# Sums of quarters of h from kept norm products, four more seven-product blocks, and one modulation vector computed a section earlier, in a two-layer hybrid decoder trunk

## The chip, the cores and the metric

The kernel runs on one core of one Trainium2 chip. A core has a matrix engine (TensorE, "PE" in the profile), a vector engine (VectorE, "DVE"), ScalarE ("ACT"), GpSimd ("POOL") and a sync engine ("SP") that here only issues DMAs. Each engine works through its own instructions in program order, and semaphores hold it where it needs another engine's result. The metric is the device time of one execution in microseconds (us).

## What is computed

Two decoder layers of 1024 features over 512 tokens, in float32, and a last norm. Each layer is a feed-forward half step, a mixer and another feed-forward half step; every one of the six has a norm with a shift and a scale that come from the conditioning vector `c`:

```python
mod = (cond @ ada_w[i] + ada_b[i]).reshape(bn, N_SUBLAYERS, 3, D_MODEL)
h = modulate(rms_norm(x, ffn_norm[i, 0]), mod[:, 0, 0], mod[:, 0, 1])   # h*(1+scale)+shift
x = x + 0.5 * mod[:, 0, 2][:, None, :] * swiglu(h, w_gate, w_up, w_down)
# swiglu: (silu(h @ w_gate) * (h @ w_up)) @ w_down, 1024 -> 2816 -> 1024
```

The mixer of layer 0 is a convolution module, that of layer 1 pooling and block attention. The change touches the four feed-forwards. They are called l0s0, l0s2, l1s0 and l1s2 here, after layer and place in the layer. There are 18 modulation vectors of 1024, each a product of `cond` with 4 MB of `ada_w`.

## The kernel before

**Products.** TensorE takes operands of a shorter float (`fp32r`). A float32 product is made from three: each operand is split into an upper part (`whi`, `hh`, `th`) and a rest (`wlo`, `hl`, `tl`), and `mac` (lines 302 to 304) multiplies upper by upper, upper by rest, rest by upper. Weights come by DMA into `raw`; ScalarE casts the upper part (line 284, `whi`) and VectorE subtracts (line 286, `wlo`). In the convolution module some items carry the flag `by_dma`: there ScalarE writes the upper part of `-w` into `wlo` (line 289), and GpSimd issues a DMA that adds `w` to it (line 290), so that VectorE has nothing to do. An *item* is 128 output features over all 512 tokens: for gate and up 8 x 3 = 24 matmuls of 512 columns.

**Sections and blocks.** The 22 blocks of 128 hidden features are done in sections of 8, 6 and 8: gate and up products of a section, then its share of the down product, which is added to `x` (line 1010). A gate block and its up block are two items. Some of them, the last ones of their section, are done together as a *pair* instead: h is cut in quarters (features by tokens), and seven products of quarter size take the place of eight (`pair_run`, `seventh`, line 791), 7 x 12 = 84 matmuls of 256 columns. The numbers of pairs in the three sections are (0, 2, 8) in l0s0, (2, 6, 8) in l0s2, (2, 4, 8) in l1s0 and (2, 6, 8) in l1s2. A pair needs sums of its weights' quarters (`sums13`, `sum2`, `sum4`, their splits; the first pair's are made ahead, in `lead_in`), a few steps on its results, and four sums of quarters of h, which `forms` makes once for each feed-forward, for `kk` = 0 to 3: two additions `hh + hl` of 512 columns into `s13` (line 730) give h back, four steps of 256 columns make the sums (lines 734 to 737), and ScalarE and VectorE split them (lines 741 and 742).

**Modulation vectors.** One vector takes four loads of 1 MB, on VectorE one TENSOR_SCALAR (line 485) and seven SCALAR_TENSOR_TENSOR (line 487) of 128x1024 into `adaacc`, a fold (two transposes and two reductions, lines 500 and 501), one small matmul and `put_mod`. These steps are a list `bg`; `slack` and `beside` put them between items, by estimated costs: each item adds a credit (`free` less the cost of what else stands beside it), and a step is placed when the credit covers it. What is left at the end is done there. `steps` builds the list of a feed-forward.

**Boundaries.** Between two steps, `boundary` takes the last two down items of the old step, the norm and the first items of the new one (the next three or four, whose operands are split early), by halves of 256 tokens. VectorE adds each finished output into `x` (line 1010) and its square into `acc` (line 543); when all eight are in, TensorE sums `acc` over the partitions (`stats`, line 553), and after VectorE and GpSimd have made the scale from that, TensorE spreads it (line 564). `apply` then makes, for each of eight row blocks, `t = x * modA * scale` (line 575, in three turning buffers), `hh` from `t + modB` (ScalarE, line 578) and `hl` (VectorE, line 580). The boundary behind l0s2 has number 3.

Of the kernel before, what the change touches and what calls it, by code (L numbers as in the profile page):

```python
# [68 lines left out]
class Trunk:  # L69
    def __init__(self, ctx, tc, a, out):  # L70
        self.ctx, self.tc, self.nc, self.a, self.out = ctx, tc, tc.nc, a, out
        self.plan = []
        self.later, self.held = [], []
        self.pend = None
        self.ending = False
        self.phase = None
        self.free_banks = list(range(8))
        self.bank_no = {}
# [263 lines left out]
    def setup(self):  # L342
# [224 lines left out]
    def apply(self, i, k, sl, rb):  # L567

        nc = self.nc
        n = sl.stop - sl.start  # L570
        if n == S:
            t = self.fp.tile([P, n], F32, name=f"t{n}", tag="qhi", bufs=3)
        else:
            t = self.np_.tile([P, n], F32, name=f"t{n}", tag="t", bufs=3)
        nc.vector.scalar_tensor_tensor(t, self.x[k][:, sl], self.modA[:, i, k:k + 1],  # L575
                                       rb, op0=ALU.mult, op1=ALU.mult)
        b = self.modB[:, i, k:k + 1]
        nc.scalar.activation(self.hh[k][:, sl], t, AF.Identity, bias=b, scale=1.0)  # L578
# [9 lines left out]
    def boundary(self, tail, i, head, switch=True):  # L588
# [74 lines left out]
    def ffn_items(self, l, s):  # L663
# [8 lines left out]
        for n, nf in enumerate(SECTIONS):  # L672
            gu = []
            for fp in range(nf // 2):
# [7 lines left out]
                def up_post(slot):  # L682
                    def go(ps, sl):
# [8 lines left out]
                c0 = (f0 + 2 * fp) * P  # L692
                apart = (l, s, n, fp) == (0, 0, 0, 1)
                sl_ = (2 * fp, 2 * fp + 1)
                g = self.pair(wg[:, :, c0:c0 + 256], ND, [gate_post(q) for q in sl_], rhs=self.h_rhs,
                              apart=apart)
                u = self.pair(wu[:, :, c0:c0 + 256], ND, [up_post(q) for q in sl_], rhs=self.h_rhs,
                              apart=apart)
                gu += [g[0], u[0], g[1], u[1]]
# [24 lines left out]
    def forms(self, kk):  # L724

        nc = self.nc
        h = self.fp.tile([P, 2, S], F32, name="s13", tag="s13", bufs=1)
        for e in range(2):
            k = kk + 4 * e
            nc.vector.tensor_tensor(h[:, e, :], self.hh[k].bitcast(F32), self.hl[k].bitcast(F32), op=ALU.add)  # L730
        b11, b12 = h[:, 0, 0:256], h[:, 0, 256:512]
        b21, b22 = h[:, 1, 0:256], h[:, 1, 256:512]
        t = [self.fp.tile([P, S], F32, name="yy", tag="yy", bufs=2).rearrange("p (a b) -> p a b", a=2) for _ in range(2)]
        nc.vector.tensor_tensor(t[0][:, 0, :], b12, b11, op=ALU.subtract)
        nc.vector.tensor_tensor(t[0][:, 1, :], b22, t[0][:, 0, :], op=ALU.subtract)
        nc.vector.tensor_tensor(t[1][:, 0, :], b12, b22, op=ALU.subtract)
        nc.vector.tensor_tensor(t[1][:, 1, :], b21, t[0][:, 1, :], op=ALU.subtract)
        for e in range(2):
# [229 lines left out]

    def swiglu_pairs(self, secs, pairs, bg, skip, fn=None, due=0):


        self.form, self.credit, self.room = {}, 0.0, len(bg)
        end = len(bg) - due
        forms = [(lambda kk=kk: self.call(lambda: self.forms(kk)), 4.6) for kk in range(4)]
        lead = [list(zip(self.lead_in(ps[0]), (2.5, 1.4, 1.9, 1.2))) if ps else [] for ps in pairs]
        for n, ((gu, down), ps) in enumerate(zip(secs, pairs)):
# [3 lines left out]
            if n == 0 and ps:  # L980
                todo = forms + [(None, 0)] * (len(gu) - 8) + todo
            rest = self.beside(gu, todo, bg, 3.7, len(ps) > 0) if gu else rest
# [18 lines left out]
        self.plan.append(("sync",))  # L1001
        while bg:
            self.call(*bg.pop(0)[:2])
            self.call(self.flush)
# [542 lines left out]
    def build(self):  # L1547
# [97 lines left out]

        bg = steps(1, (0, 1), (0, 0), (0, 2))
        self.swiglu_pairs(g0, self.pair_items(0, 2, (2, 6, 8)), bg, 3)
        self.boundary(g0[-1][1][6:], 3, f[1, 0][0][0][:4], False)
        bg = steps(1, (1, 1), (1, 0), (1, 2), (2, 1))
        self.swiglu_pairs(f[1, 0], self.pair_items(1, 0, (2, 4, 8)), bg, 3, AF.Exp)  # L1650

# [130 lines left out]
```

## Time and profile before

| | us |
|---|---|
| median of 3 runs | 1843.25 |
| lowest and highest | 1841.98, 1844.58 |
| the profiled execution, its own time | 1845.38 |
| its span in the profile | 1843.6 |
| TensorE busy | 1794.6 (97%) |
| VectorE busy | 1411.1 (77%) |
| ScalarE busy | 816.1 (44%) |
| GpSimd busy | 144.5 (8%) |

The profiled execution's own time is its span and 1.8 us around it. All stretches, waits and durations below are read in that one execution. A busy share is an average over the whole program; for each stage the waits and the timeline of that stage say more.

### The profile page before, as it was taken

The page shows a single profiled execution, that of the slowest core. Times are in us where ns is not written, and L with a number is a line of the kernel's source. Part 1 is how long each engine was busy: PE and PEld are TensorE (multiplying, and loading weights), DVE is VectorE, ACT ScalarE, POOL GpSimd, SP SyncE. Part 2 cuts the span into 40 slices and gives each one's busy share as a digit, 9 for nine tenths or more (in the row PEclk, how much of TensorE's full clock was granted, in tenths as well). Part 3 has the DMA queues.
Part 4 walks back from the last instruction along what each step waited for, and adds up shares of the span by engine and source line. Part 5 has one row for each costly group of instructions (what it writes and reads, how often), then busy time and mean ns, then how long its engine had stood idle before and what let it go on. Part 6 is the DMA issues. An engine that isn't in the chain of part 4 may idle for free.

```text
span 1843.6 us, 26711 instructions
## 1 busy us (share of the span) xinstructions
PE 1794.6 (97%) x10730; PEld 1563.4 (85%) x10730; DVE 1411.1 (77%) x2084; ACT 816.1 (44%) x1404; POOL 144.5 (8%) x123
## 2 busy tenths in 40 slices
PE   5999999999999999999999999999999999999998
PEld 3787889988778888989888889998866788898997
DVE  6689879775797869799677787886898586485874
ACT  4322325447754433436344234453545444253543
POOL 2100000005760000000000000000002000000000
PEclk7999999999999999999999999999999999999999
DMA  9585564447752346353423664543462132424321
GB/s 253 164 295 205 172 187 122 138 115 164 166 177 88 115 162 196 123 148 105 160 71 113 218 210 136 145 133 97 134 205 71 54 92 69 114 81 126 92 92 46
DMA packets 275940, 255.93 MB, mean 139 GB/s; under 512 B 5628, under 2 KB 254312, under 8 KB 275816
## 3 DMA queue, kind: packets, MB, share of 16 engines
q1 hardware_dynamic: 273380, 245.78, 43.5%
q0 software_dynamic: 2304, 8.39, 2.5%
q8 instruction: 84, 1.38, 0.3%
q14 instruction: 40, 0.33, 0.1%
q10 hardware_dynamic: 132, 0.05, 0.0%
HBM read 243.72 MB, written 2.10 MB: 133 GB/s over the span
## 4 chain that ended last, share of the span: by engine, by line
PE 81%; DVE 10%; ACT 3%; issue 2%; POOL 2%; DMA 1%; SPq 0%; ACTq 0%; POOLq 0%; DVEq 0%
PE bank L791 30%; PE bank L302 16%; PE bank L304 16%; PE bank L303 16%; DVE hl L580 1%; DVE wlo L286 1%; DVE adaacc L487 1%; DMA raw<-in_ada_w_dram 1%; ACT whi L284 1%; DVE t L575 1%; POOL y L1124 1%; DVE pm L1362 1%; DVE x L1010 1%; DVE p L1359 0%; DVE acc L1524 0%
## 5 line engine op out<-in xcount | busy, mean ns | idle before, releaser
L302 PE MATMUL bank<-th,whi 128*128 128x512 f32 (+1 forms) x896 | 336.6, 376 | 0.7 <-ACT th L1404 0.7
L304 PE MATMUL bank<-th,wlo 128*128 128x512 f32 (+1 forms) x896 | 333.9, 373 | 2.7 <-POOL wlo L286 2.7
L303 PE MATMUL bank<-tl,whi 128*128 128x512 f32 (+1 forms) x896 | 333.4, 372 | 1.1 <-DVE tl L687 0.9
L302 PE MATMUL bank<-hh,whi 128*128 128x512 f32 (+1 forms) x864 | 322.1, 373 | 5.5 <-ACT hh L578 3.2
L303 PE MATMUL bank<-hl,whi 128*128 128x512 f32 (+1 forms) x864 | 316.6, 366 | 8.1 <-DVE hl L580 8.1
L304 PE MATMUL bank<-hh,wlo 128*128 128x512 f32 (+1 forms) x864 | 315.8, 366 | 3.2 <-DVE wlo L286 2.6
L284 ACT CAST whi<-raw 128x1024 fp32r<-128x1024 f32 (+1 forms) x205 | 204.4, 1012 | 135.8 <-PE bank L303 83.3
L286 DVE TENSOR_TENSOR wlo<-raw,whi 128x1024 fp32r<-128x1024 f32 (+1 forms) x179 | 209.4, 1187 | 19.1 <-ACT whi L284 18.4
L304 PEld LDWEIGHTS bank<-th,wlo 128*128 128x128 f32 x896 | 169.4, 189 | 36.1 <-POOL wlo L286 4.3
L303 PEld LDWEIGHTS bank<-tl,whi 128*128 128x128 f32 x896 | 169.6, 189 | 32.3 <-DVE tl L687 1.3
L302 PEld LDWEIGHTS bank<-th,whi 128*128 128x128 f32 x896 | 169.6, 189 | 32.0 <-ACT th L1404 0.9
L303 PEld LDWEIGHTS bank<-hl,whi 128*128 128x128 f32 x864 | 163.4, 189 | 37.9 <-DVE hl L580 9.6
L302 PEld LDWEIGHTS bank<-hh,whi 128*128 128x128 f32 x864 | 163.6, 189 | 36.9 <-ACT hh L578 3.3
L304 PEld LDWEIGHTS bank<-hh,wlo 128*128 128x128 f32 x864 | 163.7, 189 | 33.2 <-DVE wlo L286 3.7
L1010 DVE SCALAR_TENSOR_TENSOR x<-bank,modG,x 128x512 f32<-128x512 f32 (+1 forms) x124 | 85.7, 698 | 133.2 <-PE bank L304 132.3
L791 PE MATMUL bank<-f,qhi 128*128 128x256 f32 x896 | 165.3, 282 | 0.0
L791 PE MATMUL bank<-f,whi 128*128 128x256 f32 x896 | 163.0, 280 | 0.2
L748 ACT CAST qhi<-raw 128x512 fp32r<-128x512 f32 x168 | 100.7, 621 | 111.9 <-issue 77.1
L487 DVE SCALAR_TENSOR_TENSOR adaacc<-raw,cond,adaacc 128x1024 f32<-128x1024 f32 x112 | 143.7, 1283 | 2.7
L791 PEld LDWEIGHTS bank<-f,whi 128*128 128x128 f32 x896 | 137.6, 188 | 1.9 <-ACT yy L851 0.9
L791 PEld LDWEIGHTS bank<-f,qhi 128*128 128x128 f32 x896 | 138.7, 190 | 0.0
L791 PE MATMUL bank<-f,qlo 128*128 128x256 f32 x448 | 126.5, 282 | 0.2 <-DVE qlo L751 0.2
(247 smaller groups left out, 3334.8 us busy)
## 6 DMA issues: line engine op xcount, KB each, us to landing
raw<-in_ada_w_dram SPq DMA_DIRECT2D x64, 1024.0 KB, 5.0
raw<-in_ffn_w_down_dram SPq DMA_DIRECT2D x32, 1024.0 KB, 5.5
raw<-in_ffn_w_gate_dram SPq DMA_DIRECT2D x58, 512.0 KB, 4.1
raw<-in_ffn_w_up_dram SPq DMA_DIRECT2D x58, 512.0 KB, 5.3
raw<-in_ffn_w_gate_dram SPq DMA_DIRECT2D x15, 1024.0 KB, 5.4
raw<-in_ffn_w_up_dram SPq DMA_DIRECT2D x15, 1024.0 KB, 5.4
raw<-in_ffn_w_down_dram SPq DMA_DIRECT2D x16, 768.0 KB, 4.4
raw<-in_conv_w_in_dram SPq DMA_DIRECT2D x20, 512.0 KB, 5.9
```

The lines of the kernel that those rows point to most:

```text
L284: self.nc.scalar.copy(hi[:, 0:n, :], w)
L286: low = lambda eng=eng, lo=lo, hi=hi, w=w, n=n: eng.tensor_tensor(lo[:, 0:n, :], w, hi[:, 0:n, :].bitcast(F32), op=ALU.subtract)
L302: nc.tensor.matmul(ps, lhsT=it.hi[k], rhs=xh[:, sl], start=start, stop=False)
L303: nc.tensor.matmul(ps, lhsT=it.hi[k], rhs=xl[:, sl], start=False, stop=False)
L304: nc.tensor.matmul(ps, lhsT=it.lo[k], rhs=xh[:, sl], start=False, stop=stop)
L487: nc.vector.scalar_tensor_tensor(acc, r.tile[:, j, :], self.cond[:, k:k + 1], acc, op0=ALU.mult, op1=ALU.add)
L575: nc.vector.scalar_tensor_tensor(t, self.x[k][:, sl], self.modA[:, i, k:k + 1], rb, op0=ALU.mult, op1=ALU.mult)
L580: self.pend = lambda: nc.vector.scalar_tensor_tensor(self.hl[k][:, sl], t, b, self.hh[k][:, sl].bitcast(F32), op0=ALU.add, op1=ALU.subtract)
L748: self.nc.scalar.copy(hi, src)
L791: mm = lambda w, x, start=False: nc.tensor.matmul(ps, lhsT=w, rhs=x, start=start, stop=False, skip_group_check=True)
L1010: nc.vector.scalar_tensor_tensor(self.x[d][:, sl], ps[:, sl], self.modG[:, i, d:d + 1], self.x[d][:, sl], op0=ALU.mult, op1=ALU.add)
L1124: nc.gpsimd.tensor_tensor(y, y, m, op=ALU.add)
```

## The change

1. **Sums from kept products.** In the boundaries to l0s2, l1s0 and l1s2 (`i` = 2, 3, 5) `apply` leaves its eight `t` in buffers that are otherwise the places of the form tiles (`KEPT`). `forms` uses them: h is `t + modB`, so the additions of `hh` and `hl` go, and three of the four sums become SCALAR_TENSOR_TENSOR with `modB`, or with the difference of two of its columns (`modD`, made once). l0s0 stays as it is.
2. **Four more pairs.** l1s0 has (2, 6, 8) and l1s2 has (4, 6, 8).
3. **The order in l1s2's section 0.** With four pairs only 8 items are left there, 3 of which the boundary takes. `joint` puts the forms and the lead-in steps, nine in all, beside the five others.
4. **`by_dma` in l1s2.** The four items of the second weight pair of that section get their lower parts from ScalarE and an adding DMA, as in the convolution module.
5. **One vector in another part.** The scale of layer 1's mixer (vector 1, 1 of layer 1) leaves l1s0's list and joins l0s2's, at its end. What of it is not placed by the end of l0s2 is carried over (`over`).
6. The estimated cost of a form is 3.5 in place of 4.6 where the forms come from kept products.

```diff
+        elif self.keep:
+            if sl.start == 0:
+                self.tt[k] = self.fp.tile([P, S], F32, name=f"t{k}", tag=SPARE[KEPT[k]], bufs=1)
+            t = self.tt[k][:, sl]
...
+        self.call(lambda: (setattr(self, "keep", i in (2, 3, 5)), setattr(self, "fi", i)))
...
+                by_dma = (l, s, n, fp) == (1, 2, 0, 1)
...
+                for it in g + u:
+                    it.by_dma = by_dma
...
+        if self.keep:
+
+            if kk == 0:
+                nc.vector.tensor_tensor(self.modD, self.modB[:, self.fi, 0:4], self.modB[:, self.fi, 4:8],
+                                        op=ALU.subtract)
+            (b11, b12), (b21, b22) = ([self.tt[kk + 4 * e][:, h] for h in HALVES] for e in range(2))
+            b2, bd = self.modB[:, self.fi, kk + 4:kk + 5], self.modD[:, kk:kk + 1]
+            nc.vector.tensor_tensor(t[0][:, 0, :], b12, b11, op=ALU.subtract)
+            for out, x, b, y in ((t[0][:, 1, :], b22, b2, t[0][:, 0, :]), (t[1][:, 0, :], b12, bd, b22),
+                                 (t[1][:, 1, :], b21, b2, t[0][:, 1, :])):
+                nc.vector.scalar_tensor_tensor(out, x, b, y, op0=ALU.add, op1=ALU.subtract)
...
+    def joint(self, forms, lead, n):
+
+        over = len(forms) + len(lead) - n
+        if over <= 0:
+            return forms + lead
+        forms = [forms[:2]] + [[f] for f in forms[2:]]
+        steps = [[f] for f in lead]
+        for e in range(over - 1):
+            steps[e].insert(0, forms.pop(e - over + 1)[0])
...
-                todo = forms + [(None, 0)] * (len(gu) - 8) + todo
+                todo = self.joint(forms + [(None, 0)] * (len(gu) - 8), todo, len(gu))
...
-        while bg:
+        while bg and not over:
...
-        bg = steps(1, (0, 1), (0, 0), (0, 2))
-        self.swiglu_pairs(g0, self.pair_items(0, 2, (2, 6, 8)), bg, 3)
+        bg = steps(1, (0, 1), (0, 0), (0, 2), (1, 1))
+        self.swiglu_pairs(g0, self.pair_items(0, 2, (2, 6, 8)), bg, 3, over=True)
         self.boundary(g0[-1][1][6:], 3, f[1, 0][0][0][:4], False)
-        bg = steps(1, (1, 1), (1, 0), (1, 2), (2, 1))
-        self.swiglu_pairs(f[1, 0], self.pair_items(1, 0, (2, 4, 8)), bg, 3, AF.Exp)
+        bg += steps(1, (1, 0), (1, 2), (2, 1))
+        self.swiglu_pairs(f[1, 0], self.pair_items(1, 0, (2, 6, 8)), bg, 3, AF.Exp)
...
-        self.swiglu_pairs(f[1, 2], self.pair_items(1, 2, (2, 6, 8)), [], 3)
+        self.swiglu_pairs(f[1, 2], self.pair_items(1, 2, (4, 6, 8)), [], 3)
```

The first place where instructions move is the end of l0s2, on VectorE, ahead of boundary 3. `x0_93` to `x7_100` are the eight row blocks of the output, `adaacc` and `yy` belong to the vectors in the list, `acc` to the norm. Before, behind the first output:

```order
L1010 SCALAR_TENSOR_TENSOR x1_94<-bank6_8327,modG_157,x1_94 128x512
L487 SCALAR_TENSOR_TENSOR adaacc_7141<-raw_8127,cond_151,adaacc_7141 128x1024 x2
L543 TENSOR_TENSOR acc_158<-acc_158,sq_8358 128x512
L286 TENSOR_TENSOR wlo_8366<-raw_8246,whi_8365 128x1024
L286 TENSOR_TENSOR wlo_8370<-raw_8246,whi_8369 128x1024
L1010 SCALAR_TENSOR_TENSOR x2_95<-bank7_8373,modG_157,x2_95 128x512
L500 STREAM_TRANSPOSE yy_8404<-adaacc_7141 128x512
L501 TENSOR_REDUCE adar_8403<-yy_8404 128x16
L500 STREAM_TRANSPOSE yy_8407<-adaacc_7141 128x512
L501 TENSOR_REDUCE adar_8403<-yy_8407 128x16
L543 TENSOR_TENSOR acc_158<-acc_158,sq_8399 128x512
L286 TENSOR_TENSOR wlo_8412<-raw_8248,whi_8411 128x1024
```

and from the fifth to the seventh output, whose first half is the last row:

```order
L1010 SCALAR_TENSOR_TENSOR x4_97<-bank1_8448,modG_157,x4_97 128x512
L543 TENSOR_TENSOR acc_158<-acc_158,sq_8474 128x512
L286 TENSOR_TENSOR wlo_8480<-raw_8291,whi_8479 128x1024
L1010 SCALAR_TENSOR_TENSOR x5_98<-bank5_8483,modG_157,x5_98 128x512
L543 TENSOR_TENSOR acc_158<-acc_158,sq_8509 128x512
L524 TENSOR_TENSOR modG_157<-bank3_8511,adabT_150 32x8 x4
L528 TENSOR_SCALAR modG_157<-modG_157 128x8
L286 TENSOR_TENSOR wlo_8520<-raw_8362,whi_8519 128x1024
L1010 SCALAR_TENSOR_TENSOR x6_99<-bank0_8523,modG_157,x6_99 128x256
```

After, behind the first output:

```order
L1048 SCALAR_TENSOR_TENSOR x1_94<-bank6_8313,modG_157,x1_94 128x512
L503 STREAM_TRANSPOSE yy_8347<-adaacc_6273 128x512
L504 TENSOR_REDUCE adar_8346<-yy_8347 128x16
L503 STREAM_TRANSPOSE yy_8350<-adaacc_6273 128x512
L504 TENSOR_REDUCE adar_8346<-yy_8350 128x16
L546 TENSOR_TENSOR acc_159<-acc_159,sq_8344 128x512
L288 TENSOR_TENSOR wlo_8355<-raw_8113,whi_8354 128x1024
L288 TENSOR_TENSOR wlo_8359<-raw_8113,whi_8358 128x1024
L1048 SCALAR_TENSOR_TENSOR x2_95<-bank7_8362,modG_157,x2_95 128x512
L488 TENSOR_SCALAR adaacc_8392<-raw_8232,cond_151 128x1024
L490 SCALAR_TENSOR_TENSOR adaacc_8392<-raw_8232,cond_151,adaacc_8392 128x1024
L490 SCALAR_TENSOR_TENSOR adaacc_8392<-raw_8234,cond_151,adaacc_8392 128x1024 x2
```

and from the fifth to the seventh:

```order
L490 SCALAR_TENSOR_TENSOR adaacc_8392<-raw_8390,cond_151,adaacc_8392 128x1024 x2
L490 SCALAR_TENSOR_TENSOR adaacc_8392<-raw_8395,cond_151,adaacc_8392 128x1024 x2
L546 TENSOR_TENSOR acc_159<-acc_159,sq_8472 128x512
L288 TENSOR_TENSOR wlo_8486<-raw_8399,whi_8485 128x1024
L1048 SCALAR_TENSOR_TENSOR x5_98<-bank3_8489,modG_157,x5_98 128x512
L503 STREAM_TRANSPOSE yy_8518<-adaacc_8392 128x512
L504 TENSOR_REDUCE adar_8517<-yy_8518 128x16
L503 STREAM_TRANSPOSE yy_8521<-adaacc_8392 128x512
L504 TENSOR_REDUCE adar_8517<-yy_8521 128x16
L546 TENSOR_TENSOR acc_159<-acc_159,sq_8515 128x512
L288 TENSOR_TENSOR wlo_8526<-raw_8474,whi_8525 128x1024
L1048 SCALAR_TENSOR_TENSOR x6_99<-bank0_8529,modG_157,x6_99 128x256
```

So two 128x1024 steps and one fold of before (the fold of the third vector) have become eight such steps (the whole fourth vector) and two folds, in the same stretch of TensorE's work, ahead of the norm's sums. Between the two pieces, behind `x3_96`, stand the steps of `modG`, which before stood behind `x5_98`.

The second place is ScalarE in l1s2's section 0, where the last half outputs of the boundary's items (`sg`, `th0_117`) meet the weights of the items behind it. Before:

```order
L578 ACTIVATE hh6_107<-t256_13934,modB_156 128x256
L578 ACTIVATE hh7_108<-t256_13953,modB_156 128x256
L284 CAST whi_13985<-raw_13293 128x1024
L679 ACTIVATE sg_13900<-bank2_13791 128x256
L686 CAST th0_117<-m_14007 128x256
L284 CAST whi_14011<-raw_13350 128x1024
L284 CAST whi_14015<-raw_13604 128x1024
L679 ACTIVATE sg_13912<-bank4_13813 128x256
L284 CAST whi_14023<-raw_13350 128x1024
L686 CAST th1_118<-m_14052 128x512
```

After:

```order
L286 CAST whi_14065<-raw_13378 128x1024
L687 ACTIVATE sg_13984<-bank2_13879 128x256
L694 CAST th0_117<-m_14088 128x256
L286 CAST whi_14092<-raw_13435 128x1024
L291 ACTIVATE wlo_14093<-raw_13435 128x1024
L286 CAST whi_14097<-raw_13690 128x1024
L291 ACTIVATE wlo_14098<-raw_13690 128x1024
L687 ACTIVATE sg_13996<-bank4_13901 128x256
L286 CAST whi_14106<-raw_13435 128x1024
L291 ACTIVATE wlo_14107<-raw_13435 128x1024
L694 CAST th1_118<-m_14136 128x512
```

Three `wlo` steps have come in between, each with a DMA that GpSimd issues behind it; the four subtractions of line 286 are gone from VectorE. Over the whole program TensorE has 192 matmuls of 512 columns fewer and 336 of 256 columns more.

## Rows read from the trace of the kernel before

**Rows 1.** The page: the span, the busy time of each engine (share of the span, instructions), and the chain of work that ended last, by engine.

```profile
span 1843.6 us, 26711 instructions
...
PE 1794.6 (97%) x10730; PEld 1563.4 (85%) x10730; DVE 1411.1 (77%) x2084; ACT 816.1 (44%) x1404; POOL 144.5 (8%) x123
...
PE 81%; DVE 10%; ACT 3%; issue 2%; POOL 2%; DMA 1%; SPq 0%; ACTq 0%; POOLq 0%; DVEq 0%
```

**Rows 2.** The waits of TensorE over the whole span, three groups of the list: the line that waited, what it waited for, us in total, how often, the longest.

```profile
PE bank L303 <- DVE hl L580: 8.1, 6, 1.6
...
PE bank L304 <- POOL wlo L286: 2.7, 1, 2.7
...
PE bank L304 <- DMA wlo<-raw: 0.7, 1, 0.7
```

**Rows 3.** TensorE's timeline in an ordinary item of 24 matmuls of 512 columns: its first matmul and the first one of the next item (start us, duration us, line, operation, output and inputs, shape).

```profile
601.88 0.39 PE L302 MATMUL bank<-hh,whi 128*128 128x512 f32 x1
...
607.48 0.39 PE L302 MATMUL bank<-hh,whi 128*128 128x512 f32 x1
```

**Rows 4.** The chain of work in order of time: the run of seven-product matmuls of 256 columns in section 1 of layer 1's first feed-forward (start us, us, what, how many).

```profile
1171.54 71.58 PE bank L791 x612
```

**Rows 5.** Busy time by stretch (length, busy us of each engine with its instructions, granted TensorE clock, DMA share, GB/s). The first three run from the end of section 0's products to the end of section 2's, in l0s2, l1s0 and l1s2; the fourth is the end of l0s2, from its two first finished outputs to the first half output.

```profile
682.93:784.08 101.15, 101.15 (x687) 93.01 (x686) 85.22 (x110) 42.23 (x75) 0.00 (x0) 1.00 0.51 156
1035.16:1139.61 104.45, 104.41 (x617) 91.73 (x616) 86.97 (x110) 36.92 (x61) 0.00 (x0) 1.00 0.59 192
1582.08:1683.00 100.92, 100.92 (x685) 92.78 (x684) 68.00 (x88) 42.21 (x75) 0.00 (x0) 1.00 0.34 94
899.28:926.55 27.27, 27.27 (x138) 22.79 (x137) 20.45 (x28) 9.47 (x12) 0.00 (x0) 1.00 0.36 116
```

**Rows 6.** VectorE's timeline at the end of l0s2, the start of that fourth stretch, its middle and the step after it. The bracket is the idle time before the instruction and what ended it.

```profile
899.28 1.45 DVE L1010 SCALAR_TENSOR_TENSOR x<-bank,modG,x 128x512 f32<-128x512 f32 x2 [6.61 <-PE bank L304]
900.65 2.60 DVE L487 SCALAR_TENSOR_TENSOR adaacc<-raw,cond,adaacc 128x1024 f32<-128x1024 f32 x2
...
906.70 0.71 DVE L500 STREAM_TRANSPOSE yy<-adaacc 128x512 f32<-128x512 f32 x1
...
908.78 0.69 DVE L501 TENSOR_REDUCE adar<-yy 128x16 f32<-128x512 f32 x1
...
911.18 0.75 DVE L1010 SCALAR_TENSOR_TENSOR x<-bank,modG,x 128x512 f32<-128x512 f32 x1
912.70 0.69 DVE L543 TENSOR_TENSOR acc<-acc,sq 128x512 f32<-128x512 f32 x1 [0.76 <-ACT sq L539]
...
922.38 0.75 DVE L1010 SCALAR_TENSOR_TENSOR x<-bank,modG,x 128x512 f32<-128x512 f32 x1 [1.92 <-PE bank L304]
...
926.55 0.48 DVE L1010 SCALAR_TENSOR_TENSOR x<-bank,modG,x 128x256 f32<-128x256 f32 x1
...
929.10 0.42 DVE L543 TENSOR_TENSOR acc<-acc,sq 128x256 f32<-128x256 f32 x1 [0.55 <-ACT sq L539]
```

**Rows 7.** VectorE's groups by line and shape between 580 and 1840 us (count, busy us, mean ns of one, idle before).

```profile
L487 DVE SCALAR_TENSOR_TENSOR adaacc<-raw,cond,adaacc 128x1024 f32<-128x1024 f32 x63 | 80.8, 1283 | 1.5
...
L575 DVE SCALAR_TENSOR_TENSOR t<-x,modA,bank 128x256 f32<-128x256 f32 x64 | 29.6, 474 | 0.0
...
L730 DVE TENSOR_TENSOR s<-hh,hl 128x512 f32<-128x512 f32 x24 | 15.4, 684 | 0.0
...
L485 DVE TENSOR_SCALAR adaacc<-raw,cond 128x1024 f32<-128x1024 f32 x9 | 6.7, 747 | 0.0
```

**Rows 8.** TensorE's timeline right behind the fourth stretch: the matmuls of the norm's sums of squares, and the ones that bring its scale to all partitions.

```profile
929.91 0.50 PE L553 MATMUL bank<-ones,acc 128*128 128x1 f32 x4
...
931.51 0.43 PE L564 MATMUL bank<-ident,rs 128*128 128x128 f32 x2
```

**Rows 9.** One lower part that is made by ScalarE and an adding DMA, in the conv module: ScalarE's two steps, GpSimd's issue, the matmul that used it, and the summary of line 290 (16 such DMAs).

```profile
424.42 1.04 ACT L284 CAST whi<-raw 128x1024 fp32r<-128x1024 f32 x1
425.35 1.06 ACT L289 ACTIVATE wlo<-raw 128x1024 fp32r<-128x1024 f32 x1
...
426.75 1.06 POOL L290 DMA_DIRECT2D wlo<-raw  x1 [15.78 <-ACT wlo L289]
...
431.57 0.50 PE L304 MATMUL bank<-hh,wlo 128*128 128x512 f32 x1 [0.69 <-DMA wlo<-raw]
...
DMA to landing us min/median/max: 4.6/5.9/9.0
```

**Rows 10.** The same two places in l1s2's section 0: ScalarE's first step for the items of its second weight pair, and the third matmul of the first of these items.

```profile
1501.72 2.00 ACT L284 CAST whi<-raw 128x1024 fp32r<-128x1024 f32 x2
...
1507.10 0.39 PE L304 MATMUL bank<-hh,wlo 128*128 128x512 f32 x1
```

**Rows 11.** The lead-in of l0s2's section 1: VectorE's last step of the running block's first half (`u2`), and TensorE's next product on that block's path.

```profile
719.64 0.43 DVE L848 TENSOR_TENSOR bank<-bank,p1c 128x256 f32<-128x256 f32 x1
...
722.83 0.40 PE L791 MATMUL bank<-f,whi 128*128 128x256 f32 x2
```

**Rows 12.** TensorE's wait in front of the conv module's output products, the stretch right after it, and a stretch around a shorter wait in the next boundary (columns as in rows 5).

```profile
530.27 0.80 PE L304 MATMUL bank<-th,wlo 128*128 128x512 f32 x1 [2.66 <-POOL wlo L286]
...
529.50:536.40 6.90, 6.13 (x13) 4.14 (x14) 6.21 (x6) 3.65 (x6) 6.26 (x3) 0.51 0.45 152
581.00:584.00 3.00, 1.41 (x12) 1.21 (x12) 2.81 (x4) 0.70 (x3) 2.15 (x1) 1.00 0.00 0
```

More of the change, by code (lines that the diff above doesn't have):

```diff
@@ L30 @@
 SPARE = [f"f{i}" for i in range(16)]
+KEPT = (4, 8, 12, 14, 5, 9, 13, 15)
 HALVES = (slice(0, 256), slice(256, 512))
@@ L76, in __init__ @@
         self.phase = None
+        self.keep, self.fi, self.tt = False, 0, {}
         self.free_banks = list(range(8))
@@ L445, in setup @@
         self.modG = cp.tile([P, 6, ND], F32, name="modG")
+        self.modD = cp.tile([P, 4], F32, name="modD")
         self.acc = cp.tile([P, S], F32, name="acc")
@@ L693, in ffn_items @@
                 apart = (l, s, n, fp) == (0, 0, 0, 1)
+                by_dma = (l, s, n, fp) == (1, 2, 0, 1)
                 sl_ = (2 * fp, 2 * fp + 1)
                 g = self.pair(wg[:, :, c0:c0 + 256], ND, [gate_post(q) for q in sl_], rhs=self.h_rhs,
-                              apart=apart)
+                              apart=apart, whole=by_dma)
                 u = self.pair(wu[:, :, c0:c0 + 256], ND, [up_post(q) for q in sl_], rhs=self.h_rhs,
-                              apart=apart)
+                              apart=apart, whole=by_dma)
+                for it in g + u:
+                    it.by_dma = by_dma
                 gu += [g[0], u[0], g[1], u[1]]
@@ L726, in forms @@
         nc = self.nc
[L727 to L732, printed above, removed]
-        t = [self.fp.tile([P, S], F32, name="yy", tag="yy", bufs=2).rearrange("p (a b) -> p a b", a=2) for _ in range(2)]
-        nc.vector.tensor_tensor(t[0][:, 0, :], b12, b11, op=ALU.subtract)
@@ L735, in forms @@
-        nc.vector.tensor_tensor(t[0][:, 1, :], b22, t[0][:, 0, :], op=ALU.subtract)
-        nc.vector.tensor_tensor(t[1][:, 0, :], b12, b22, op=ALU.subtract)
-        nc.vector.tensor_tensor(t[1][:, 1, :], b21, t[0][:, 1, :], op=ALU.subtract)
+        t = [self.fp.tile([P, S], F32, name="yy", tag="yy", bufs=2).rearrange("p (a b) -> p a b", a=2) for _ in range(2)]
+        if self.keep:
[8 more added lines that the diff above has]
+                nc.vector.scalar_tensor_tensor(out, x, b, y, op0=ALU.add, op1=ALU.subtract)
+        else:
+            h = self.fp.tile([P, 2, S], F32, name="s13", tag="s13", bufs=1)
+            for e in range(2):
+                k = kk + 4 * e
+                nc.vector.tensor_tensor(h[:, e, :], self.hh[k].bitcast(F32), self.hl[k].bitcast(F32), op=ALU.add)
+            b11, b12 = h[:, 0, 0:256], h[:, 0, 256:512]
+            b21, b22 = h[:, 1, 0:256], h[:, 1, 256:512]
+            nc.vector.tensor_tensor(t[0][:, 0, :], b12, b11, op=ALU.subtract)
+            nc.vector.tensor_tensor(t[0][:, 1, :], b22, t[0][:, 0, :], op=ALU.subtract)
+            nc.vector.tensor_tensor(t[1][:, 0, :], b12, b22, op=ALU.subtract)
+            nc.vector.tensor_tensor(t[1][:, 1, :], b21, t[0][:, 1, :], op=ALU.subtract)
@@ L967, in beside, with both, swiglu_pairs @@
         return rest
-    def swiglu_pairs(self, secs, pairs, bg, skip, fn=None, due=0):
+    def joint(self, forms, lead, n):
[6 more added lines that the diff above has]
+            steps[e].insert(0, forms.pop(e - over + 1)[0])
+        def both(fs):
+            return lambda: [f[0]() for f in fs]
+        return [(both(fs), sum(f[1] for f in fs)) for fs in forms + steps]
+    def swiglu_pairs(self, secs, pairs, bg, skip, fn=None, due=0, over=False):
         self.form, self.credit, self.room = {}, 0.0, len(bg)
         end = len(bg) - due
-        forms = [(lambda kk=kk: self.call(lambda: self.forms(kk)), 4.6) for kk in range(4)]
+        forms = [(lambda kk=kk: self.call(lambda: self.forms(kk)), 4.6 if fn == AF.Sigmoid else 3.5) for kk in range(4)]
         lead = [list(zip(self.lead_in(ps[0]), (2.5, 1.4, 1.9, 1.2))) if ps else [] for ps in pairs]
```

## The prediction

> **What bounds the kernel now.** I read the page first. TensorE is busy for 1794.6 of 1843.6 us, and it holds 81% of the chain of work that ended last [rows 1]. So a matmul that goes is time that goes, as long as nothing makes TensorE wait instead. The list of TensorE's waits is next: it is short, and in the feed-forwards its one repeated entry is the wait for the first `hl` of a boundary, 1.6 us at the longest [rows 2]. Then come the stretches of the three feed-forwards that the change touches: TensorE fills them wholly, and VectorE is busy for 85.22 of 101.15, 86.97 of 104.45 and 68.00 of 100.92 us [rows 5]. VectorE's work is therefore hidden there on average. It matters where much of it stands together in front of something that TensorE needs, and the places to look for that are the boundaries, where the norm is a chain through VectorE: outputs, squares, sums, scale. So I read VectorE's timeline in front of boundary 3, which the change loads [rows 5, 6], and the precedent of the adding DMA [rows 9].
>
> **The pairs.** An item is 24 matmuls of 512 columns and takes 607.48 - 601.88 = 5.60 us, 233 ns each [rows 3]. Matmuls of 256 columns follow each other at 71.58 / 612 = 117 ns [rows 4]. A pair takes 84 x 0.117 = 9.83 us in place of 11.20, so it saves 1.37. For the two pairs in l1s2 that is 2.7. For those in l1s0 there is a direct row: the same stretch takes 104.45 us with four pairs and 101.15 with six [rows 5], a difference of 3.3, and l1s0 will have the six. Together -6.0 us. What a pair adds on VectorE lies under products that keep TensorE at work in the same stretches, as it does with six pairs now.
>
> **The kept products.** Each of the three feed-forwards loses eight additions of 0.684 us on VectorE, and three of the four 256-column steps of a form become SCALAR_TENSOR_TENSOR, like the ones of line 575 at 0.474 us [rows 7]. That is some 5 us of VectorE time for each feed-forward, and TensorE waits for none of it now. I cost it at nothing, gain or loss: its worth is that the same steps fit beside five items in l1s2 where nine stood. There a form is two splits of 512 columns, at most 0.684 us each like line 730, and four steps of 256, at most 0.474 [rows 7]: 3.3 us. Four of them, and the first pair's lead-in with some seven steps of 128x1024 at 1.2 us or less, are an estimated 21.5 us of VectorE, and the five items give 5 x 5.60 = 28 us, some 24 of them behind the boundary's last steps. If that cover were gone, each us over it would be a us of wait.
>
> **The vector at the end of l0s2.** VectorE's list here comes in the order of the program. In the stretch of 27.27 us it is busy for 20.45, so 6.82 are idle [rows 5]. It has two 128x1024 steps and one fold, which runs from 906.70 to 909.38, 2.68 us [rows 6]. With the change there are one TENSOR_SCALAR (0.747), seven of the other kind (1.283 each [rows 7]) and two folds: 0.75 + 5 x 1.28 + 2.68 = 9.8 us more. The idle time can't all be used: after an output VectorE must still wait for ScalarE's square, 0.76 us at 912.70 [rows 6], and by my replay of the new order one such wait stays. So the first half output (`x6`, 926.55) comes 9.8 - 6.8 + 0.8 = 3.8 us late, 3.7 in the replay step by step. What is queued behind it on VectorE is the rest of the norm's sum: now its last addition ends at 929.52 and TensorE takes up the sums at 929.91 without a wait [rows 6, 8]; after, it ends at about 933.2. TensorE's own queue holds everything else behind those matmuls. I take **+3.3 us**; the ends are 0, if the steps ran earlier than I place them, and 4.1, if a second such wait of 0.76 stays.
>
> **The clock after it.** In front of the conv module's output TensorE waited for 2.66 us, and in the following 6.9 us its granted clock was 0.51, the lower of its two levels [rows 12]. Around a 1.6 us wait in a boundary it stayed at 1.00 [rows 12]. A wait of 3.3 us is nearer to the first. Here the matmuls between the sums and the spread (929.91 to 931.51 [rows 8]) would take twice as long, and behind that the wait for `hl` of 1.6 us takes up the rest of the delay. I take **+1.1**; the ends are 0 and 3.4, which is half of a stretch of 6.9 us. The Trainium skill (TensorE: Matmul & The Clock Gate, Part 1: The HAM clock gate) says that the lower level is the default and that activity releases it; the fall after 2.66 us and the level of 1.00 after 1.6 us in this trace agree, and the sum above stands without it.
>
> **The adding DMA in l1s2.** In the conv module the chain for one lower part is: `whi` on ScalarE at 424.42, `wlo` at 425.35, the issue at 426.75, and the matmul that needed it at 431.57, which waited [rows 9]. From the start of `whi` to the use are 7.15 us. In l1s2 the same item's `whi` starts at 1501.72, and its third matmul, the first to read `wlo`, is due at 1507.10 [rows 10]. So it would come at 1508.87, **+1.8 us**. That DMA landed after 4.8 us; with the least of the 16 it is 1.6, with their median of 5.9 it is 2.9 [rows 9], and the low end is 0, if the item stands later than I think. The other three DMAs have one or more items of 5.6 us of room. What goes from VectorE (four subtractions) was hidden. The Trainium skill (DMA: Bandwidth & Descriptors, Anatomy of one DMA — SWDGE (gpsimd) path) fits such a DMA with 2.0 us and bytes at 436 GB/s, an estimate of 3.2 us for 512 KB; by it the wait would be about 0.2 us and the sum 1.6 lower. The rows, from 4.6 us up, are longer, and they decide.
>
> **The small ones.** In l0s2's section 1 the list is fuller, and by the new order a fold stands ahead of the first block's `u2`, which comes some 2.2 us later. It runs at 719.64 and TensorE's next product on its path starts at 722.83, 2.8 us after its end [rows 11], of which ScalarE's two copies need 0.8: **+0.2**. GpSimd, which gets four DMAs more, is busy for 8% of the span [rows 1]. The sixteen 1 MB loads of the vectors are as many as before.
>
> **Sum.** -6.0 + 3.3 + 1.1 + 1.8 + 0.2 = +0.4 us. It is made against the profiled execution, 1845.38 us, which would become 1845.8. That execution lies 2.1 us above the median of the runs shown, so the median goes from 1843.25 to **1843.7**.
>
> **The rivals.**
> - *A, both waits come (the forecast)*, with the clock's cost from 0 to 2: from 1842.3 to 1845.5. For it: the order is fixed, and its length is a sum of rows. 0.62.
> - *B, no wait at boundary 3.* VectorE would have to find 3 us more, for instance if these steps ran before the stretch, in the 6.61 us in which it waits for the first output [rows 6]. Against it: the program has them behind that output. Then -6.0 + 1.8 + 0.2 = -4.0, 1839.2, faster. 0.10.
> - *C, the adding DMA is in time*, but boundary 3 waits: 0.4 - 1.8 = -1.4, 1841.9, within 0.2%. Speaking for it: the conv module ran its loads beside the adding DMAs, and in l1s2 the DMA load is the lightest of the three stretches, 0.34 [rows 5]. 0.12.
> - *D, neither wait*: -6.0 + 0.2 = -5.8, 1837.5. 0.07. This is what the change does if it does what its counts say and VectorE's order costs nothing.
> - *E, the clock stays low (slower).* After the wait at boundary 3 the lower level lasts through the boundary's first products. Without the clock the sum is -0.7, so slower by 0.2% (+3.7) begins at 4.4 us of loss, 8.8 us at half rate; after the wait before the conv output it was 6.9 [rows 12], and the boundary's `hl` wait, just behind, would have to keep it down. With 10 us at half rate it is -0.7 + 5 = +4.3, 1847.6. 0.09.
> - That the kept products give TensorE nothing is part of A; if l1s2's section 0 overran by VectorE's 21.5 us against 24, it would show as a wait in front of its first pair, and I leave 1 us for it in the range.
>
> **How the numbers follow.** What a measurement of this kernel can tell from no change is about 0.2%, 3.7 us. Faster by more takes B or D, and a part of C's low end: 0.19. Slower is E, and a little of A where the DMA takes 2.9 us or more and the clock 3.4: 0.10. The rest, 0.71, is the same. The range leaves out D below and the tail of E above, 1838.8 to 1847.0.
>
> **What would show it.** Right: 5.5 to 6 us less of TensorE's matmul time between section 0 and the last section of l1s0 and l1s2; a new wait of 3 to 4 us of the sums' matmul for VectorE's `acc` in boundary 3, and the granted clock under 1.00 just behind it; a wait of about 1.8 us for a DMA's `wlo` some 6 us after the boundary into l1s2; no new wait in front of a form's first use. Wrong: no wait for `acc` there (the vector's steps were hidden, B or D), a DMA that landed in time (C), or a fall of the clock over the whole boundary (E). If the pairs saved less than 1.2 us each, the first term is wrong.

## The result, and the profile after

The changed kernel takes 1854.89 us (median of 6 runs, 1854.42 to 1855.27), the kernel before 1843.05 (6 runs): 1.0064 times as long, 95% interval 1.0051 to 1.0077. That is 11.8 us slower. The prediction was 1843.7 us, no difference, from 1838.8 to 1847.0: wrong.

The page of the profiled execution (1855.27 us): the span and the busy times.

```profile
span 1853.4 us, 27069 instructions
...
PE 1800.6 (97%) x10874; PEld 1575.8 (85%) x10874; DVE 1415.7 (76%) x2091; ACT 830.8 (45%) x1436; POOL 147.9 (8%) x127
```

TensorE has 6.0 us more busy time than before [rows 1], where the change should have taken 5.5 us of matmuls from it. So the loss isn't one long wait. Four groups from the list of TensorE's waits, after (the line that waited, what it waited for, us in total, how often, the longest), agree:

```profile
PE bank L305 <- DVE hl L587: 7.7, 6, 1.5
...
PE bank L306 <- POOL wlo L288: 4.6, 3, 2.4
...
PE bank L304 <- DVE x L1048: 2.3, 1, 2.3
...
PE bank L306 <- DMA wlo<-raw: 1.9, 2, 1.4
```

Two waits are new, 2.3 us for an output `x` and 1.4 us for an adding DMA, and the prediction has a wait at both places; 12 us are not in the list. The stretches of rows 5, after, with the same columns and cut at the same outputs:

```profile
686.42:788.35 101.93, 101.93 (x687) 93.49 (x686) 87.29 (x114) 42.38 (x75) 0.00 (x0) 1.00 0.49 155
1044.21:1146.03 101.82, 101.82 (x687) 93.57 (x686) 85.25 (x111) 42.38 (x75) 0.00 (x0) 1.00 0.45 145
1590.36:1691.97 101.61, 101.61 (x685) 93.36 (x684) 67.88 (x89) 42.38 (x75) 0.00 (x0) 1.00 0.31 94
904.36:935.11 30.75, 29.00 (x149) 24.26 (x147) 29.53 (x39) 9.46 (x12) 0.00 (x0) 1.00 0.60 205
```

In l1s0 the two pairs save time (104.45 to 101.82 us). But the first and the third stretch have the same matmuls as before, no waits, and the same granted clock, and take 101.93 and 101.61 us in place of 101.15 and 100.92 [rows 5]. The chain shows it best. The run of 612 seven-product matmuls took 71.58 us before [rows 4]; after, it reads:

```profile
1178.05 72.18 PE bank L814 x612
```

All four such runs of the program read 72.18, in l0s0 too, to whose code nothing was done. So the matmuls themselves follow each other more slowly. I worked out the mean time from the start of one matmul to the start of the next from the traces, from 140 us on, leaving out every gap of 1.4 times the usual or more: at 256 columns it is 116.57 ns before and 117.85 after (6275 of them), at 512 columns 232.61 and 233.49 (3608). That is 6275 x 1.28 + 3608 x 0.88 ns = 8.0 + 3.2 = 11.2 us of the 11.8.

What could do that everywhere? The new tile `modD` stands in the middle of the constants: 16 bytes that take 32, so `acc`, `raw`, `whi`, `wlo` and all tiles of the phase (`t`, `f`, `yy`, `qhi`, `qlo`) lie 32 bytes further on, while `x`, `hh`, `hl`, `th` and `tl` stay. Theory P (for place) says that where these tiles lie sets how fast matmuls follow each other. Its rival L (for load) says that the new order puts other work beside the matmuls and that this slows them.

### The profile page after: what moved, and what is told of

Same layout as the page of the kernel before. It is cut to its first block, busy times and chain, and to the rows that moved or that the text cites. A ratio compares the mean times of both kernels' runs of the same rounds, so it can differ in the third digit from the quotient of the medians.

```text
span 1853.4 us, 27069 instructions
## 1 busy us (share of the span) xinstructions
PE 1800.6 (97%) x10874; PEld 1575.8 (85%) x10874; DVE 1415.7 (76%) x2091; ACT 830.8 (45%) x1436; POOL 147.9 (8%) x127
## 4 chain that ended last, share of the span: by engine, by line
PE 78%; DVE 11%; issue 4%; ACT 3%; POOL 2%; DMA 1%; SPq 0%; POOLq 0%; ACTq 0%; DVEq 0%
PE bank L814 32%; PE bank L304 15%; PE bank L306 15%; PE bank L305 15%; DVE wlo L288 2%; DVE adaacc L490 2%; DVE hl L587 1%; ACT whi L286 1%; DVE x L1048 1%; POOL y L1162 1%; DVE t L582 1%; DVE pm L1400 1%; DVE acc L1562 1%; DMA wlo<-raw 0%; DVE p L1397 0%
## 5 line engine op out<-in xcount | busy, mean ns | idle before, releaser
L304 PE MATMUL bank<-hh,whi 128*128 128x512 f32 (+1 forms) x800 | 297.9, 372 | 4.6 <-ACT hh L585 2.9
L305 PE MATMUL bank<-hl,whi 128*128 128x512 f32 (+1 forms) x800 | 292.0, 365 | 7.7 <-DVE hl L587 7.7
L306 PE MATMUL bank<-hh,wlo 128*128 128x512 f32 (+1 forms) x800 | 291.5, 364 | 3.8 <-DMA wlo<-raw 1.9
L288 DVE TENSOR_TENSOR wlo<-raw,whi 128x1024 fp32r<-128x1024 f32 (+1 forms) x167 | 195.0, 1185 | 18.0 <-ACT whi L286 17.0
L305 PEld LDWEIGHTS bank<-hl,whi 128*128 128x128 f32 x800 | 151.9, 190 | 34.9 <-DVE hl L587 9.3
L304 PEld LDWEIGHTS bank<-hh,whi 128*128 128x128 f32 x800 | 151.8, 190 | 33.1 <-ACT hh L585 2.9
L306 PEld LDWEIGHTS bank<-hh,wlo 128*128 128x128 f32 x800 | 151.7, 190 | 31.6 <-DVE wlo L288 3.1
L814 PE MATMUL bank<-f,qhi 128*128 128x256 f32 x960 | 176.9, 282 | 0.0
L814 PE MATMUL bank<-f,whi 128*128 128x256 f32 x960 | 174.6, 280 | 0.0
L814 PEld LDWEIGHTS bank<-f,whi 128*128 128x128 f32 x960 | 147.4, 188 | 1.6 <-ACT yy L874 0.7
```

Source lines behind the costliest of these rows:

```text
L288: low = lambda eng=eng, lo=lo, hi=hi, w=w, n=n: eng.tensor_tensor(lo[:, 0:n, :], w, hi[:, 0:n, :].bitcast(F32), op=ALU.subtract)
L304: nc.tensor.matmul(ps, lhsT=it.hi[k], rhs=xh[:, sl], start=start, stop=False)
L305: nc.tensor.matmul(ps, lhsT=it.hi[k], rhs=xl[:, sl], start=False, stop=False)
L306: nc.tensor.matmul(ps, lhsT=it.lo[k], rhs=xh[:, sl], start=False, stop=stop)
L814: mm = lambda w, x, start=False: nc.tensor.matmul(ps, lhsT=w, rhs=x, start=start, stop=False, skip_group_check=True)
```

## Experiments: the place of the tiles

**`modD` in free columns.** The changed kernel, with every tile at its address of before:

```diff
-        self.modD = cp.tile([P, 4], F32, name="modD")
...
-        self.ms = [cp.tile([P, 4], F32, name=f"ms{i}") for i in range(2)]
+        ms = [cp.tile([P, 8], F32, name=f"ms{i}") for i in range(2)]
+        self.ms, self.modD = [t[:, 0:4] for t in ms], ms[0][:, 4:8]
```

> The changed kernel, with modD in four free columns behind ms0's four, so that every tile behind it has its address of before. Theory P (the places of the tiles set how fast matmuls follow each other): 256-column matmuls back from 117.85 to about 116.6 ns, 512-column ones from 234.3 to about 233.3, and the time to about 1843 us. Rival L (the load beside the matmuls, by the new order, slows them): 1855 us, rates as in the changed kernel.

Measured: 1842.92 us, 0.9997 (0.9988 to 1.0007) of before. All else of the change is in it. The mean distances are 116.44 and 232.60 ns. P holds, L falls. (The 234.3 and 233.3 ns of the expectation are those of 512-column matmuls among their like: from one matmul of `hh` or `hl` past `whi` or `wlo` to the next, with two more of these before and behind, the mean is 234.24 ns in the changed kernel and 233.32 here.)

**The kernel before with an unused tile** of 32 bytes at that place (`e2`), behind the weight splits (`e3`), or both (`e5`):

```diff
+        self.pad = cp.tile([P, 4], F32, name="pad")      # e2, e5: ahead of acc
+        self.nc.vector.memset(self.pad, 0.0)
...
+        npad = self.np_.tile([P, 4], F32, name="npad", tag="npad", bufs=1)      # e3, e5
+        nc.vector.memset(npad, 0.0)
```

> The kernel before, with an unused tile of 4 columns where modD stands, which moves every tile behind it by 32 bytes. Theory P: about 1854 us (11 us more), 256-column matmuls at about 117.9 ns. Rival L: 1843 us, rates of before.

> The kernel before, with the unused tile behind the weight splits, so that only the tiles of the norm and of the phase (t, f, yy, qhi, qlo) move by 32 bytes. Theory P with the weight splits whi and wlo as the cause: within 2 us of 1843. With the phase's tiles as the cause: 1850 us or more. Rival L: 1843 us.

> The kernel before, with one unused tile at modD's place and one behind the weight splits: raw, whi and wlo move by 32 bytes, the phase's tiles by 64. Theory P with whi and wlo as the cause: 1850 us or more, hh x whi of 256 columns at 117.5 ns in place of 115. With the phase's tiles as the cause: about 1843. Rival L: 1843 us.

Measured: 1855.11 (1.0063, 1.0048 to 1.0078), 1846.31 (1.0017, 1.0008 to 1.0027) and 1856.00 us (1.0064, 1.0049 to 1.0079). An unused tile alone gives the whole loss of the change, and it comes when the weight parts move (`e2`, `e5`). Moving the phase's tiles alone (`e3`) costs some 3 us, of which the matmuls of its profiled execution show about 1; the rest stays open. `acc` and `raw` move with the weight parts in all of these kernels and were not moved alone. The chain of `e2`:

```profile
1178.56 72.18 PE bank L793 x612
```

**Whose place?** Unused tiles ahead of `x` alone (`h1`: all move by 32), ahead of `x` and at `modD`'s place (`h3`: h by 32, the rest by 64), and one of 64 bytes at `modD`'s place (`h2`):

```diff
+        xpad = cp.tile([P, 4], F32, name="xpad")      # h1, h3: ahead of x
+        nc.vector.memset(xpad, 0.0)
...
+        self.pad = cp.tile([P, 16], F32, name="pad")      # h2: ahead of acc; h3: [P, 4]
+        self.nc.vector.memset(self.pad, 0.0)
```

> The kernel before, with an unused tile of 32 bytes ahead of x, so that x, h, th, tl, the weights and all behind move by 32 bytes together. Theory P1 (what counts is whether a weight part and the tile that streams past it stand alike within 64 bytes): h and weights move together, so 1843 us and hh x whi of 256 columns at 115 ns. Theory P2 (the weights' own place within 64 bytes counts): 1855 us, 117.5 ns, as with the shift at modD's place.

> The kernel before, with unused tiles of 32 bytes ahead of x and at modD's place: x, h, th, tl move by 32 bytes, the weights and the phase's tiles by 64. P1 (alike or not): 1853 us or more, hh x whi of 256 columns at 117.5 ns. P2 (the weights' own place): 1843 us, 115 ns.

> The kernel before, with an unused tile of 64 bytes at modD's place: everything behind it moves by 64 bytes. P1 and P2 alike, as both count within 64 bytes: 1843 us, 256-column matmuls at 116.6 ns. If any move of these tiles costs, or the longer distance does: 1850 us or more.

Measured: 1843.06 (0.9997, 0.9988 to 1.0006), 1853.47 (1.0056, 1.0041 to 1.0072) and 1853.41 us (1.0053, 1.0040 to 1.0067). The chains of `h1`, `h3` and `h2`:

```profile
1168.66 71.58 PE bank L793 x612
```

```profile
1175.89 72.18 PE bank L795 x612
```

```profile
1175.35 72.65 PE bank L793 x612
```

`h1` moves `x` and all behind it and reads as before, `h3` reads as `e2`, with which it shares the distance of 32 bytes more between h and the rest. So what counts is how far tiles lie from each other, and not the place of any one of them: that is one half of P1. Its other half, "within 64 bytes", fell with `h2`.

Which tiles these are shows in the matmuls of h past `whi` and `wlo` among their like, worked out as for `e1`. At 512 columns they read 233.32 ns in the kernel before, `e1` and `e3` and 233.31 in `h1`, 234.25 in `e2` and `e5` and 234.26 in `h3`, and 232.69 in `h2`. So the distance from h to the weight parts (0, 32 and 64 bytes more) sets them, wherever the phase's tiles lie. At 256 columns that isn't all. Among the seven products these matmuls go from 113.67 ns before to 117.38 in `e2` and 117.35 in `h3`, but also to 115.35 in `e3`, where neither h nor these weight parts moved. They stand between groups that stream `f` or read `qhi` and `qlo`, which did move; how one group acts on the next stays open.

**Which distance.** The best kernel below (`h4`), with unused tiles of 96 to 224 bytes at `modD`'s place:

```diff
+        pad = cp.tile([P, 32], F32, name="pad")      # i1; 24, 48, 40, 56 columns in the others
+        self.nc.vector.memset(pad, 0.0)
```

> h4_best with an unused tile of 128 bytes at modD's place. If the distance between h and the weights counts within 128 bytes: 1837.5 us as h4_best, 256-column matmuls at 116.5 ns. If within a longer period, or any other distance is worse: 1845 us or more, 117.8 ns or more.

> h4_best with an unused tile of 96 bytes there. With a period of 128 this is 32 bytes less than before; the rows so far have 32 more (11.5 us slower) and 64 more (10 us slower), so a kernel that is slower by about as much is likeliest, 1848 us; a time near 1837 would say that only one side of the distance is bad.

> h4_best with an unused tile of 192 bytes there. With a period of 128 the same as 64 more: 1847 us, 256-column matmuls at 118.6 ns and 512-column ones at 231.9 ns, as in h2_shift64. Other rates would mean a longer period.

> h4_best with an unused tile of 160 bytes at modD's place. If the rates go smoothly with the distance, between 128 and 192: 512-column matmuls at about 228 ns, 256-column ones at about 118 ns, 1829 us. If the odd multiples of 32 are bad ones (32 and 96 were): 1840 us or more.

> h4_best with an unused tile of 224 bytes there. If the rates go smoothly: 512-column matmuls near 227 ns as at 192, time about 1830 us. If odd multiples of 32 are bad ones: 1840 us or more.

| distance more than before, bytes | from | 256 columns, ns | 512 columns, ns | us | ratio to before |
|---|---|---|---|---|---|
| 0 | h4 | 116.47 | 232.53 | 1837.46 | 0.9967 |
| 32 | e2 | 117.91 | 233.50 | 1855.11 | 1.0063 |
| 64 | h2 | 118.62 | 231.94 | 1853.41 | 1.0053 |
| 96 | i2 | 118.70 | 232.68 | 1849.74 | 1.0031 |
| 128 | i1 | 117.46 | 228.76 | 1828.97 | 0.9918 |
| 160 | j160 | 117.74 | 232.65 | 1844.71 | 1.0001 |
| 192 | i3 | 118.53 | 227.15 | 1829.95 | 0.9927 |
| 224 | j224 | 117.62 | 232.57 | 1843.64 | 0.9997 |

(The distance is the one from h to the weight parts; the phase's tiles move with these. Rows 32 and 64 stand on the kernel before, the others on `h4`, 5.7 us faster by itself.) The times are neither smooth in the distance nor of a period of 64 or 128 bytes, and the two sizes don't go together. `i1` came out faster than either branch of its expectation, and `i3` is far from the 1847 us of a period of 128 bytes. The second branch of the last two expectations came true: at the odd multiples of 32 the long matmuls gain nothing, and none of these four kernels is faster than before by more than its interval. At 128 bytes the long matmuls gain 3.77 ns x 3600 = 13.6 us and the short ones lose 0.99 x 6278 = 6.2. `i1` is the fastest kernel here, 0.9918 (0.9900 to 0.9935) of before, though `i3` (0.9911 to 0.9943) can't be told from it. Its 512-column items are 5.49 us apart in the down products of l1s2, where those of `h4` are 5.60 apart, as in [rows 3]. Two outputs in a row of `i1`, then of `h4`:

```profile
1577.75 0.75 DVE L1050 SCALAR_TENSOR_TENSOR x<-bank,modG,x 128x512 f32<-128x512 f32 x1 [3.37 <-PE bank L306]
1583.24 0.75 DVE L1050 SCALAR_TENSOR_TENSOR x<-bank,modG,x 128x512 f32<-128x512 f32 x1 [3.36 <-PE bank L306]
```

```profile
1585.52 0.75 DVE L1048 SCALAR_TENSOR_TENSOR x<-bank,modG,x 128x512 f32<-128x512 f32 x1 [3.48 <-PE bank L306]
...
1591.12 0.75 DVE L1048 SCALAR_TENSOR_TENSOR x<-bank,modG,x 128x512 f32<-128x512 f32 x1 [3.48 <-PE bank L306]
```

The short ones are slower, as the chain of `i1` shows:

```profile
1160.00 72.23 PE bank L816 x612
```

What in the memory makes a distance good is not settled.

## Experiments: the terms of the sum

**Half of the vector left to l1s0** (from here on all with `e1`'s `modD`):

```diff
-        while bg and some < 2 and self.credit >= bg[0][2] and (self.room > 0 or bg[0][1] is None):
+        while len(bg) > self.stop and some < 2 and self.credit >= bg[0][2] and (self.room > 0 or bg[0][1] is None):
...
+        self.form, self.credit, self.room, self.stop = {}, 0.0, len(bg), 6 if over else 0
```

> As e1_modd_in_gap, but the second half of the moved vector (four steps of 128x1024 and the fold) is left to l1s0, so that the end of l0s2 carries 4 such steps and one fold in place of 8 and two. Theory (VectorE's order in front of boundary 3 makes TensorE wait): boundary 3 3.3 us shorter than in e1, time about 1839.6 us. Rival (something else in that boundary costs the 3.3 us, or l1s0's end now gets the wait): about 1843 us.

Measured: 1838.55 us, 0.9968 (0.9958 to 0.9978). VectorE's timeline at boundary 3 in the changed kernel, where the last row is the first half output:

```profile
911.94 0.75 DVE L488 TENSOR_SCALAR adaacc<-raw,cond 128x1024 f32<-128x1024 f32 x1
912.73 3.93 DVE L490 SCALAR_TENSOR_TENSOR adaacc<-raw,cond,adaacc 128x1024 f32<-128x1024 f32 x3
...
923.14 5.24 DVE L490 SCALAR_TENSOR_TENSOR adaacc<-raw,cond,adaacc 128x1024 f32<-128x1024 f32 x4
...
935.11 0.48 DVE L1048 SCALAR_TENSOR_TENSOR x<-bank,modG,x 128x256 f32<-128x256 f32 x1
```

TensorE waits for that last step, because it needs the bank that the step frees. That wait, and the stretch behind it (columns as in rows 5):

```profile
935.64 0.38 PE L304 MATMUL bank<-th,whi 128*128 128x256 f32 x1 [2.28 <-DVE x L1048]
```

```profile
936.00:940.00 4.00, 4.00 (x34) 3.72 (x33) 1.89 (x5) 0.51 (x2) 0.70 (x1) 1.00 0.00 0
```

In `g1` the same wait is gone, and the first half output comes at 925.75, 26.92 us after the first output:

```profile
898.83 1.45 DVE L1048 SCALAR_TENSOR_TENSOR x<-bank,modG,x 128x512 f32<-128x512 f32 x2 [6.62 <-PE bank L306]
...
925.75 0.48 DVE L1048 SCALAR_TENSOR_TENSOR x<-bank,modG,x 128x256 f32<-128x256 f32 x1
```

From the first output of l0s2's end to that of l1s0's section 0, `g1` takes 3.33 us less than `e1`. The medians are 4.4 us apart; the difference of 1 us is within their intervals and was not followed up.

**No adding DMA in l1s2** (`f2`, on top of `e1`), and **the first of its four lower parts on VectorE** (`g2`, on top of `g1`):

```diff
-                by_dma = (l, s, n, fp) == (1, 2, 0, 1)
+                by_dma = False      # f2
...
-                for it in g + u:
+                for it in g[1:] + u:      # g2
```

> The changed kernel with the addresses of before (as e1_modd_in_gap), and the four items of l1s2's second weight pair with their lower parts from VectorE again. If the adding DMA's wait (about 1.5 us in e1's trace) is its whole effect: l1s2 from boundary to boundary 1.5 us shorter than in e1, time about 1841.5 us. If VectorE then comes late with the forms (four subtractions of 1.2 us on top of 21.5 us where about 24 are free): a wait of about 2 us in front of the section's first pair, time about 1843.5 us.

> As g1_split_vector, and the first of the four items with an adding DMA gets its lower part from VectorE. Theory (only the first DMA lands late): 1.5 us less than g1, about 1838 us, no wait for a DMA's wlo in l1s2. Rival (the next DMA is late as well, or the 1.2 us on VectorE come back in front of the first pair): as g1.

Measured: `f2` 1840.67 us, 0.9985 (0.9975 to 0.9994), with l1s2's start 1.84 us shorter than in `e1` by the first outputs; `g2` 1837.50, 0.9965 (0.9952 to 0.9978), with the same part 1.55 us shorter than in `e1`. The wait of the changed kernel, which is gone in both:

```profile
1517.65 0.50 PE L306 MATMUL bank<-hh,wlo 128*128 128x512 f32 x1 [1.38 <-DMA wlo<-raw]
```

In `f2` VectorE makes all four parts beside the forms and nothing waits for it.

**The kept products alone** (`f3`): the counts, lists and splits of before (`(2, 4, 8)`, `(2, 6, 8)`, the vector in l1s0, `by_dma = False`).

> The counts of pairs, the vector lists and the splits of before; only the sums of quarters come from the kept products, with modD in free columns so that every address in front of the phase's tiles is that of before. If VectorE's shorter forms are hidden: 1843 us, no difference to before. If the kept tiles cost or give something by themselves: over 2 us away.

Measured: 1844.67 us, 1.0002 (0.9993 to 1.0012): nothing, as forecast.

**Both together** (`h4`): `g1` with `by_dma = False`.

> g1_split_vector without the adding DMA in l1s2: addresses of before, half of the moved vector left to l1s0, VectorE makes all lower parts. By the terms measured apart (boundary 3 3.3 us shorter, l1s2 1.8 us shorter than in e1): 1837 to 1838 us, 6 us under the kernel before. If VectorE's four subtractions come back as a wait beside the full list: 1839 us or more.

Measured: 1837.46 us, 0.9967 (0.9954 to 0.9979), better than both kernels; with 128 bytes more it is `i1`.

## Why the prediction was wrong

The step that failed is "a matmul that goes is time that goes": the part on the pairs took 233 and 117 ns from the trace of before and let every matmul keep that pace. The kept products, which bring `modD`, were put "at nothing, gain or loss" by their work on VectorE alone, and no term stood for the place that `modD` takes. Its 32 bytes slow the matmuls of the whole program and cost 1854.89 - 1842.92 = 12.0 us, shown by `e1` from one side and `e2` from the other.

With that term out (`e1`), the steps of the sum can be read one by one, by the times of the first outputs in the traces of before and `e1`:
- Pairs, -6.0: right. l1s0's stretch is 3.30 us shorter. The start of l1s2 is 1.22 us shorter with the DMA's wait in it, and 3.05 shorter in `f2`, without it.
- The vector, +3.3: right in size, 3.3 from the first output of l0s2's end to that of l1s0's section 0. The replay of VectorE put the first half output 3.7 us late; in the changed kernel it came 30.75 - 27.27 = 3.5 late. The waiting instruction was an earlier one than the prediction names: not the sums, but the matmul that needed the bank of that output.
- The clock, +1.1: wrong. It stayed at 1.00 behind the wait of 2.28 us in boundary 3, and behind 2.54 us there in `e1`. The prediction set the wait beside the one of 2.66 us in front of the conv module's output [rows 12], but the length of that wait doesn't decide: in the same place of `f3` TensorE waited 2.65 us, and the clock stayed at 1.00 in the 6.9 us behind it.

```profile
529.70 0.50 PE L306 MATMUL bank<-th,wlo 128*128 128x512 f32 x1 [2.65 <-POOL wlo L288]
```

```profile
529.70:536.60 6.90, 4.66 (x19) 3.21 (x20) 6.21 (x6) 3.65 (x6) 5.48 (x2) 1.00 0.52 161
```

- The adding DMA, +1.8: 1.4 to 1.8. The matmul waited 1.38 us in the changed kernel and 1.55 in `e1`; without the DMA 1.84 go. The Trainium skill (DMA: Bandwidth & Descriptors, Anatomy of one DMA — SWDGE (gpsimd) path) fits a DMA on this path with 2.0 us and its bytes at 436 GB/s, from which the prediction's estimate of a 0.2 us wait came. The traces don't agree for the adding DMA, which takes 4.6 us or more from issue to landing [rows 9]; the conv module's row was the better guide.
- The lead-in of l0s2's section 1, +0.2: its stretch is 0.23 us longer.
- The kept products, 0: right for the work that they change, by `f3`, which has `modD` in free columns; wrong for the tile that they bring.

These terms, as read in `e1`, add up to -1.0 us, where the sum says +0.4, and -0.7 without the clock. The medians put `e1` at -0.2 us (0.9988 to 1.0007). So with the tile out of the way the time lies in the stated range, and not by luck: of the sum's terms only the clock's is wrong in size. Rivals B to D fell with `g1` and `f2`, E with the clock. The bounds of rival A don't follow from its own terms: with 0 to 2 us for the clock the sum gives 1842.5 to 1844.6 us, and not 1842.3 to 1845.5.

## What to carry to other kernels

Before you cost a change, list what it allocates as well as what it runs. A new tile moves all tiles behind it; one of 16 bytes cost this kernel 12 us, and it hid a change that is worth 5.7 when its two waits are taken out (`h4`). Where matmuls fill the time, read a run of equal matmuls in the chain (71.58 and 72.18 us for 612). If it differs in code that was not touched, look at addresses before looking for waits, and try an unused tile in the kernel before. Read each size of matmul by itself: the fastest kernel here, `i1`, gains on its long matmuls, and its run of 612 short ones takes 72.23 us. Put new constants in free columns of tiles that are there, as `e1` does, and try a few distances between weights and streamed tiles: here the best of eight was worth 8.5 us.

## What was not expected of the hardware

- The time from one matmul to the next depends on how far the weights' tiles lie from the tiles that stream past them: 256 columns take from 116.5 to 118.7 ns, 512 columns from 227.2 to 233.5 ns, over eight distances 32 bytes apart. Moving both together changed nothing (`h1`: 71.58 us for 612 again).
- The two sizes have their best at different distances (0 and 192 bytes more).
- Two waits of nearly the same length in the same place, 2.66 us in the kernel before [rows 12] and 2.65 in `f3`, were followed by a granted clock of 0.51 in the one execution and of 1.00 in the other.
